# HGRN2's level loop: the second operand of each product copied by ScalarE, q multiplied beside k; retention's fourfold copies in one instruction

## The chip, the core and the metric

The kernel runs on one core of a Trainium2 chip. A core has five engines that run side by side and meet at semaphores: TensorE (PE, matrix products; its weight loads are shown apart as PEld), VectorE (DVE), ScalarE (ACT), GpSimd (POOL) and SyncE (SP, which here issues the transfers between the main memory and the core). The metric is the time of one execution on the device in microseconds; of several runs the median is taken.

## The reference

One step of a decoder trunk with two layers, width 2048, over 256 prompt tokens and 8 sequences of 4 sample tokens each; the kernel treats them as 288 columns. Layer 0 mixes by retention (4 heads) beside an RG-LRU, layer 1 by HGRN2 (16 heads of 128). After each mixer and each convolutional FFN stands a layer norm. For one HGRN2 head the reference computes, with `fg` the forget gate and `k = 1 - fg`:

```python
S_t = diag(f_t) S_{t-1} + k_t v_t^T ;  o_t = S_t^T q_t
# in chunks, b = cumsum(log f):
A = einsum('bhtk,bhsk,bhtsk->bhts', q, k, exp(b_t - b_s))      # s <= t
o = einsum('bhts,bhsv->bhtv', A, v) + einsum('bhtk,bhkv->bhtv', q * exp(b), S)
```

Retention computes `(q k^T * decay) v + q S` in the same way with a fixed decay for each head, and a new state. All inputs and outputs are float32.

## The kernel before

**Products.** Activations lie feature by feature: 16 tiles of 128 features by 288 columns. The weights stream from the main memory in chunks of 16 tiles of 128x128. ScalarE rounds half a chunk (8 tiles, 128x1024) to a high part `wh`, VectorE subtracts to get the low part `wl` (`split_hi`, `split_lo`); both are made some chunks of 8 ahead of their use. `gemm` sends three products for a weight tile (high by high, high by low, low by high) of 288 columns each.

**Order of the work.** The order of each engine's instructions is that in which the program is written, for TensorE, VectorE, ScalarE and GpSimd. The work of the heads is written as generators. After each weight tile `gemm` calls `tasks.tick()`, which lets one due generator go on; `yield n` means: not before n further ticks. So the distance between two steps of a head, in weight tiles on TensorE, is what stands in the `yield`s (`GAP_A`, `GAP_B`, `STAGE`), or more where several generators are due at once. An engine that has to wait for a semaphore holds up all that is written behind it on that engine.

**HGRN2's levels.** The triangle of a head's decayed scores `A` is built in seven levels, L = 1, 2, 4 to 64, after its diagonal. At level L the columns stand in blocks of 2L. Keys of a block's early half meet queries of its late half. Both have been multiplied with the gates between them and the block's middle, and the totals `T` of the gates are halved in number at each level. The prompt's second chunk of 128 columns runs backwards, so that one product serves both chunks. In a level (`levels`):

- `gather(i)`: ScalarE copies the early halves of k into the packed tile `E` (128x128).
- `scores(i)`: TensorE multiplies `E` with the late halves of q, read in place with a strided pattern (`late_half`), into a PSUM tile `hl`. At L = 2 a small second product serves the sample columns.
- VectorE multiplies k's early halves by the totals, makes the next totals `T`, and, after `yield GAP_A`, multiplies q's late halves (L1291); both in place.
- `keep(i)`: VectorE copies the valid scores under a mask into `AA` (L1255). Then comes `gather(i + 1)`, then `yield GAP_B + slow`, where `slow` is 1 in heads 0 and 1 and otherwise 0.

Since q is multiplied in place, VectorE may do it only when the product has read it, and the next product needs it done. After the levels follow transposes, state products and the output product `hpo`, which reads `AA`. A head takes 48 weight tiles (64 from head 7 on, where the gate's product stands beside it), so in heads 0 to 7 the tail of a head runs beside the levels of the next.

**Retention.** `vals` and `ret_inner` write the 32 sample columns of values and keys four times side by side into `v4` and `k4` on GpSimd, by four copies of 128x32 for each of two tiles; transposes on TensorE (`pst`) read them.

Of the kernel before, what the change touches and what calls it, by code (L numbers as in the profile page):

```python
# [10 lines left out]
F32 = mybir.dt.float32  # L11
F32R = mybir.dt.float32r
U32 = mybir.dt.uint32
AF = mybir.ActivationFunctionType
ALU = mybir.AluOpType
# [3 lines left out]
P = 128  # L19
D = 2048  # L20
KT = D // P
TP = 256
NB = 8
NS = 4
TS = NB * NS
T = TP + TS
# [18 lines left out]
LEAD_S = 3  # L45
STAGE = 4
D0 = 8
G0 = 0
GAP_A = 2
GAP_B = 2  # L50
R0 = 14
# [154 lines left out]
def early_half(t, L):  # L206

    return bass.AP(t.tensor, t.offset, [list(t.ap[0]), [2 * L, P // (2 * L)], [P + L, 2], [1, L]])


def late_half(t, L, c_first):

    n, c = [2 * L, P // (2 * L)], [P - L, 2]
    return bass.AP(t.tensor, t.offset + L, [list(t.ap[0])] + ([c, n] if c_first else [n, c]) + [[1, L]])


def totals(t, L, late):

    nb = P // (2 * L)
    o, c = (1, 2 * nb - 1) if late else (0, 2 * nb + 1)  # L220
    return bass.AP(t.tensor, t.offset + o, [list(t.ap[0]), [2, nb], [c, 2], [0, L]])
# [31 lines left out]
def build(tc, A, phases="ACDF"):  # L253
    nc = tc.nc
    V = nc.vector
    S = nc.scalar
    G = nc.gpsimd
# [7 lines left out]
    with contextlib.ExitStack() as est:  # L265
# [9 lines left out]
        def psx(name):  # L275
            return px.tile([P, 512], F32, tag="px", name=name)

        def mm(o, l, r, start=True, stop=True):
            return nc.tensor.matmul(o, l, r, start=start, stop=stop, skip_group_check=True)  # L279

        def tr(o, i):
            return nc.tensor.transpose(o, i, ident[:, :P])
# [26 lines left out]
        class Stream:  # L309
# [5 lines left out]
            cur = {}  # L315
# [454 lines left out]
        def even_in(eo, ea, o_rg, o_rt, prev, norm):  # L770
# [49 lines left out]
            def rope(h, nm, ms):  # L820
                a = [ea.tile([P, T], F32, name=f"{nm}{i}_{h}", tag=f"{nm}{i}") for i in range(2)]
                b = [ea.tile([P, T], F32, name=f"{nm}b{i}_{h}", tag=f"rb{i}") for i in range(2)]
                for i in range(2):
                    gemm("ev_in", ks, [ms[i]], xh, xl, done=lambda m, ps: rope_a(ps, a, b, i))
                return a

            def vals(h):
                vt = [ea.tile([P, T], F32, name=f"vt{i}_{h}", tag=f"vt{i}") for i in range(2)]
                v4 = ea.tile([P, 2 * 4 * TS], F32, name=f"v4_{h}", tag="v4")
                v44 = v4.rearrange("p (n r t) -> p n r t", n=2, r=4)  # L830

                def vdone(m, ps):
                    i = m - 16 - 2 * h
                    S.activation(vt[i], ps[:, :T], AF.Copy)
                    for r in range(4):
                        G.tensor_copy(v44[:, i, r, :], vt[i][:, TP:T])

                for i in range(2):
                    gemm("ev_in", ks, [16 + 2 * h + i], xh, xl, done=vdone)
                return vt, v4  # L840
# [98 lines left out]
            with tc.tile_pool(name="rt", bufs=1) as rt:  # L939
                for h in range(H_RET):  # L940
# [9 lines left out]
                    kk = rope(h, "k", [8 + 2 * h, 9 + 2 * h]) if h else kk0  # L950
# [3 lines left out]
                    vt, v4 = vals(h) if h else vv0  # L954
# [40 lines left out]
        def ret_inner(rt, h, cv, kk, qq, hd):  # L995
            zp = cv("zp")
            k4 = rt.tile([P, 2 * 4 * TS], F32, name=f"k4_{h}", tag="k4")
            k44 = k4.rearrange("p (n r t) -> p n r t", n=2, r=4)
            for kt in range(2):
                for r in range(4):  # L1000
                    G.tensor_copy(k44[:, kt, r, :], kk[kt][:, TP:T])
            hd["k4"] = k4
            a0 = psx(f"pa0_{h}")
            a1 = psx(f"pa1_{h}")
            for kt in range(2):
                mm(a0[:, :TP], kk[kt][:, 0:P], qq[kt][:, 0:TP], start=(kt == 0), stop=(kt == 1))
            for kt in range(2):
                mm(a1[:, :P], kk[kt][:, P:TP], qq[kt][:, P:TP], start=(kt == 0), stop=(kt == 1))
            for kt in range(2):
                mm(a1[:TS, P:P + TS], kk[kt][:, TP:T], qq[kt][:, TP:T], start=(kt == 0), stop=(kt == 1))  # L1010
            hd["A0"] = A0 = rt.tile([P, TP], F32, name=f"A0_{h}", tag="A0")
            hd["A1"] = A1 = rt.tile([P, P], F32, name=f"A1_{h}", tag="A1")
            hd["As"] = As = rt.tile([TS, TS], F32, name=f"As_{h}", tag="As")
            V.tensor_tensor(A0, a0[:, :TP], cv(f"dm{h}"), op=ALU.mult)
            V.tensor_tensor(A1, a1[:, :P], cv(f"dm{h}")[:, :P], op=ALU.mult)
            V.tensor_tensor(As, a1[:TS, P:P + TS], cv(f"dms{h}")[:TS], op=ALU.mult)
            hd["qx"] = qx = [rt.tile([P, TS], F32, name=f"qx{kt}_{h}", tag=f"qx{kt}") for kt in range(2)]
            for kt in range(2):
                V.tensor_tensor(qx[kt], qq[kt][:, TP:T], cv("xi")[:, h * TS:(h + 1) * TS], op=ALU.mult)
            yield 5  # L1020
            hd["ktk"] = ktk = [rt.tile([P, 256], F32, name=f"ktk{j}_{h}", tag=f"ktk{j}") for j in range(2)]
            for j in range(2):
                pk = psx(f"pkt{h}_{j}")
                for kt in range(2):
                    tr(pk[:, kt * P:(kt + 1) * P], kk[kt][:, j * P:(j + 1) * P])
                S.activation(ktk[j], pk[:, :256], AF.Copy, scale=zp[:, 2 * h + j:2 * h + j + 1])
# [148 lines left out]
        class HG:  # L1175
# [8 lines left out]
            def tl(self, nm, shape=(P, T), dt=F32, bufs=2):  # L1184
                return self.od.tile(list(shape), dt, name=f"{nm}_{self.h}", tag=nm, bufs=bufs)
# [48 lines left out]

            def gather(self, i):

                self.e = self.od.tile([P, P], F32, name=f"E{i}_{self.h}", tag="E", bufs=3)
                cut = lambda a: a.rearrange("p (n c l) -> p n c l", c=2, l=1 << i)
                S.activation(cut(self.e), early_half(self.k, 1 << i), AF.Copy)

            def scores(self, i):

                L = 1 << i
                self.ps = ps = psx(f"hl{self.h}_{i}")
                mm(ps[:, :P], self.e, late_half(self.qc, L, True))
                if L == 2:
                    late = self.qc[:, TP:].rearrange("p (n s l) -> p n s l", s=2, l=L)[:, :, 1, :]
                    mm(ps[:, P:P + TS // 2], self.k[:, T - P:], late)
# [15 lines left out]

            def levels(self):
                h, tl, k, qc = self.h, self.tl, self.k, self.qc
                slow = 1 if h < 2 else 0
                self.AA = tl("AA", (P, TP))
                k4 = tl("hk4", (P, P))
                self.gather(0)  # L1270
# [2 lines left out]
                cur = self.f  # L1273
                for i in range(7):
                    L = 1 << i
                    self.scores(i)
                    early, late = early_half(k, L), late_half(qc, L, False)
                    V.tensor_tensor(early, early, totals(cur, L, True), op=ALU.mult)
                    W = T if L <= 2 else TP
                    nb = W // (2 * L)  # L1280
                    tv = cur[:, :2 * nb].rearrange("p (n s) -> p n s", s=2)
                    if L <= 2:
                        n0 = TP // (2 * L)
                        ks = k[:, TP:T].rearrange("p (n s l) -> p n s l", s=2, l=L)[:, :, 0, :]
                        qs = qc[:, TP:T].rearrange("p (n s l) -> p n s l", s=2, l=L)[:, :, 1, :]
                        bc = lambda j: tv[:, n0:nb, j:j + 1].to_broadcast([P, nb - n0, L])
                        V.tensor_tensor(ks, ks, bc(1), op=ALU.mult)
                    nt = tl(f"T{i}", (P, nb))
                    V.tensor_tensor(nt, tv[:, :, 0], tv[:, :, 1], op=ALU.mult)
                    yield GAP_A + (G0 if i == 0 else 0)  # L1290
                    V.tensor_tensor(late, late, totals(cur, L, False), op=ALU.mult)  # L1291
                    if L <= 2:
                        V.tensor_tensor(qs, qs, bc(0), op=ALU.mult)
                    self.keep(i)
                    if L == 2:
                        self.t4 = nt[:, TP // 4:T // 4]
                    cur = nt
                    if i < 6:
                        self.gather(i + 1)
                    yield GAP_B + slow  # L1300
                self.tot = cur
                G.tensor_copy(k4.rearrange("p (r t) -> p r t", r=4), k[:, TP:T].unsqueeze(1).to_broadcast([P, 4, TS]))
                qm = self.qms[h % 2]
# [17 lines left out]
                kt = tl("kt", (P, 2 * P))  # L1321
# [8 lines left out]
                for b in range(NB):  # L1330
                    r = slice(32 * (b % 4), 32 * (b % 4) + TS)
# [51 lines left out]
                for j in range(2):  # L1383
                    pn = psx(f"hpn{h}_{j}")
                    c = slice(j * 512, (j + 1) * 512)
# [123 lines left out]
        for ph in phases:  # L1509
            i = "ACDF".index(ph)  # L1510
# [111 lines left out]
```

## Time and profile before

| | |
|---|---|
| median of 3 runs | 2830.85 us (2830.67 to 2831.03) |
| the profiled execution | 2834.14 us, its span 2832.2 us |
| busy: PE, DVE, ACT, POOL | 98%, 62%, 45%, 20% of the span |
| weights and states from the main memory | 450.71 MB read |
| L1239 copies `E`, x112 | 35.4 us on ScalarE |
| L1291 multiplications of q by totals, x96 | 31.8 us on VectorE |

An instruction's row names its line, engine and operation, and the tile written and those read (`out<-in`, buffer numbers left out). What ended an idle time of its engine stands behind `<-`. TensorE's instructions are pipelined: one starts before the one ahead of it has ended, so lengths overlap. A float32 product is drawn as two passes.

### The profile page before, as it was taken

What the parts mean: (1) busy time and instruction counts of PE and PEld (TensorE: products, weight loads), DVE (VectorE), ACT (ScalarE), POOL (GpSimd) and SP (SyncE); (2) the same over time, 40 slices, a digit from 0 to 9 for tenths busy, and PEclk for the clock granted to TensorE, in tenths of its full rate; (3) what the DMA queues carried; (4) which work ended last, traced back from release to release, by engine and by line L of the source; (5) the groups of instructions that cost most, each with busy time, mean ns of one, the idle gap of its engine ahead of it and who ended that gap; (6) DMA issues with size and microseconds to landing.
All of it is one profiled execution on the core that took longest, in us unless ns stands there. A gap on an engine that the chain in (4) does not pass through costs nothing.

```text
span 2832.2 us, 51174 instructions
## 1 busy us (share of the span) xinstructions
PE 2786.0 (98%) x21068; PEld 2752.9 (97%) x21068; DVE 1745.1 (62%) x2683; ACT 1277.2 (45%) x2234; POOL 556.7 (20%) x975
## 2 busy tenths in 40 slices
PE   9999999999999999999999999999999999999997
PEld 9999999999999999999999999999999999999997
DVE  7665566854554554558777766676854555554556
ACT  6534445643343443445555545555643443433433
POOL 1411024510000000007332222244400000000016
PEclk9999999999999999999999999999999999999998
DMA  6465444444444445445444444444444444444442
GB/s 250 165 242 201 182 167 167 159 170 164 164 164 165 171 156 177 166 160 182 148 151 161 167 167 155 166 158 162 164 164 172 171 151 177 164 164 168 167 166 90
DMA packets 80153, 476.20 MB, mean 168 GB/s; under 512 B 9392, under 2 KB 17840, under 8 KB 28208
## 3 DMA queue, kind: packets, MB, share of 16 engines
q1 hardware_dynamic: 79920, 472.94, 46.6%
q8 instruction: 165, 2.70, 0.4%
q14 instruction: 68, 0.56, 0.1%
HBM read 450.71 MB, written 22.19 MB: 167 GB/s over the span
## 4 chain that ended last, share of the span: by engine, by line
PE 88%; DVE 6%; ACT 2%; POOL 2%; issue 1%; DMA 0%; SPq 0%; DVEq 0%; ACTq 0%; POOLq 0%
PE ps_up L279 36%; PE ps_dn L279 18%; PE ps_od_in L279 12%; PE ps_ev_in L279 9%; PE ps_ev_out L279 4%; PE ps_od_out L279 4%; DVE wl L352 2%; PE hl L279 1%; DVE xl L580 1%; ACT wh L342 1%; PE hpo L279 1%; DVE xl L415 1%; DVE x L608 1%; PE po L279 0%; PE hpS L279 0%
## 5 line engine op out<-in xcount | busy, mean ns | idle before, releaser
L352 DVE TENSOR_TENSOR wl<-wr,wh 128x1024 fp32r<-128x1024 f32 (+1 forms) x818 | 1024.4, 1258 | 145.8 <-ACT wh L342 71.5
L342 ACT ACTIVATE wh<-wr 128x1024 fp32r<-128x1024 f32 (+1 forms) x818 | 845.5, 1049 | 352.8 <-PE ps_dn L279 294.1
L279 PE MATMUL ps_up<-xl,wh 128*128 128x288 f32 (+1 forms) x2816 | 832.8, 296 | 2.7 <-DVE xl L415 2.1
L279 PE MATMUL ps_up<-xh,wh 128*128 128x288 f32 (+1 forms) x2816 | 831.6, 295 | 3.2 <-ACT vs L405 3.2
L279 PE MATMUL ps_up<-xh,wl 128*128 128x288 f32 (+1 forms) x2816 | 831.7, 295 | 0.0
L279 PEld LDWEIGHTS ps_up<-xh,wh 128*128 128x128 f32 x2816 | 530.4, 188 | 3.8 <-ACT vs L405 3.7
L279 PEld LDWEIGHTS ps_up<-xl,wh 128*128 128x128 f32 x2816 | 529.5, 188 | 4.2 <-DVE xl L415 3.1
L279 PEld LDWEIGHTS ps_up<-xh,wl 128*128 128x128 f32 x2816 | 530.8, 188 | 0.0
L279 PE MATMUL ps_dn<-hh,wh 128*128 128x288 f32 x1408 | 417.4, 296 | 0.0
L279 PE MATMUL ps_dn<-hl,wh 128*128 128x288 f32 x1408 | 416.7, 296 | 0.0
L279 PE MATMUL ps_dn<-hh,wl 128*128 128x288 f32 x1408 | 415.1, 295 | 0.0
L279 PE MATMUL ps_od_in<-xh,wh 128*128 128x288 f32 (+1 forms) x1024 | 320.1, 313 | 0.1
L279 PE MATMUL ps_od_in<-xl,wh 128*128 128x288 f32 (+1 forms) x1024 | 302.8, 296 | 2.8 <-DVE xl L415 2.8
L279 PE MATMUL ps_od_in<-xh,wl 128*128 128x288 f32 (+1 forms) x1024 | 302.3, 295 | 0.0
L1415 POOL COPY fco<-us 128x2 f32<-128x2 f32 x88 | 18.4, 209 | 1367.3 <-ACT us L403 1367.3
L279 PEld LDWEIGHTS ps_dn<-hl,wh 128*128 128x128 f32 x1408 | 265.7, 189 | 0.1
L279 PEld LDWEIGHTS ps_dn<-hh,wl 128*128 128x128 f32 x1408 | 265.8, 189 | 0.0
L279 PEld LDWEIGHTS ps_dn<-hh,wh 128*128 128x128 f32 x1408 | 265.1, 188 | 0.1
L279 PE MATMUL ps_ev_in<-xh,wh 128*128 128x288 f32 x768 | 234.2, 305 | 0.3 <-ACT wh L342 0.3
L279 PE MATMUL ps_ev_in<-xh,wl 128*128 128x288 f32 x768 | 228.3, 297 | 0.5 <-DVE wl L352 0.5
L279 PE MATMUL ps_ev_in<-xl,wh 128*128 128x288 f32 x768 | 228.3, 297 | 0.0
L279 PEld LDWEIGHTS ps_od_in<-xl,wh 128*128 128x128 f32 x1024 | 193.6, 189 | 5.0 <-DVE xl L415 3.7
(316 smaller groups left out, 3913.7 us busy)
## 6 DMA issues: line engine op xcount, KB each, us to landing
wr<-w SPq DMA_DIRECT2D x404, 1024.0 KB, 4.8
s<-sret SPq DMA_DIRECT2D x16, 512.0 KB, 6.0
rs<-s SPq DMA_DIRECT2D x16, 512.0 KB, 4.7
hs<-shg SPq DMA_DIRECT2D x16, 512.0 KB, 5.6
gs<-hs SPq DMA_DIRECT2D x16, 512.0 KB, 2.6
wr<-w SPq DMA_DIRECT2D x6, 512.0 KB, 5.9
x<-x SPq DMA_DIRECT2D x16, 144.0 KB, 5.1
y<-x SPq DMA_DIRECT2D x16, 144.0 KB, 1.8
```

Of the source, the lines that this page charges most:

```text
L279: return nc.tensor.matmul(o, l, r, start=start, stop=stop, skip_group_check=True)
L342: S.activation(hi[:, d], src, AF.Copy)
L352: V.tensor_tensor(lo[:, d], src, hi[:, d].bitcast(F32), op=ALU.subtract)
L415: (eng or V).tensor_tensor(xl[k], src, xh[k].bitcast(F32), op=ALU.subtract)
L580: V.scalar_tensor_tensor(xl[k], x[k], self.col("lng", k), xh[k].bitcast(F32), ALU.mult, ALU.subtract)
L608: (G if i in MUG else V).tensor_tensor(x[k], x[k], self.rs, op=ALU.mult)
L1415: G.tensor_copy(fc4[:, f, 0, :], s[:, TP:TP + 2])
```

## The change

In the levels, `gather` makes a second packed copy: ScalarE copies the late halves of q into a tile `L`, and `scores` multiplies `E` with `L` and reads q no more (the small product at L = 2 still reads q and k in place). So VectorE's multiplication of q stands right behind that of k. `scores(i)` moves from the beginning of a level to `GAP_A` ticks behind the gathering for the next level, except at L = 2, where it stays at the beginning; `keep(i)` moves to the end. `E` and `L` have four buffers each (before: `E` three). The extra tick of heads 0 and 1 goes. In retention the four copies become one, whose input is read four times by a pattern of step 0.

```diff
--- before.py
+++ after.py
@@ -45,7 +45,6 @@
 LEAD_S = 3
 STAGE = 4
 D0 = 8
-G0 = 0
 GAP_A = 2
 GAP_B = 2
 R0 = 14
@@ -832,8 +831,7 @@
                 def vdone(m, ps):
                     i = m - 16 - 2 * h
                     S.activation(vt[i], ps[:, :T], AF.Copy)
-                    for r in range(4):
-                        G.tensor_copy(v44[:, i, r, :], vt[i][:, TP:T])
+                    G.tensor_copy(v44[:, i], vt[i][:, TP:T].unsqueeze(1).to_broadcast([P, 4, TS]))
 
                 for i in range(2):
                     gemm("ev_in", ks, [16 + 2 * h + i], xh, xl, done=vdone)
@@ -997,8 +995,7 @@
             k4 = rt.tile([P, 2 * 4 * TS], F32, name=f"k4_{h}", tag="k4")
             k44 = k4.rearrange("p (n r t) -> p n r t", n=2, r=4)
             for kt in range(2):
-                for r in range(4):
-                    G.tensor_copy(k44[:, kt, r, :], kk[kt][:, TP:T])
+                G.tensor_copy(k44[:, kt], kk[kt][:, TP:T].unsqueeze(1).to_broadcast([P, 4, TS]))
             hd["k4"] = k4
             a0 = psx(f"pa0_{h}")
             a1 = psx(f"pa1_{h}")
@@ -1234,15 +1231,18 @@
 
             def gather(self, i):
 
-                self.e = self.od.tile([P, P], F32, name=f"E{i}_{self.h}", tag="E", bufs=3)
-                cut = lambda a: a.rearrange("p (n c l) -> p n c l", c=2, l=1 << i)
-                S.activation(cut(self.e), early_half(self.k, 1 << i), AF.Copy)
+                L = 1 << i
+                self.e[i], self.l[i] = [self.od.tile([P, P], F32, name=f"{n}{i}_{self.h}", tag=n, bufs=4) for n in "EL"]
+                cut = lambda a: a.rearrange("p (n c l) -> p n c l", c=2, l=L)
+                S.activation(cut(self.e[i]), early_half(self.k, L), AF.Copy)
+                cut = lambda a: a.rearrange("p (c n l) -> p c n l", c=2, l=L)
+                S.activation(cut(self.l[i]), late_half(self.qc, L, True), AF.Copy)
 
             def scores(self, i):
 
                 L = 1 << i
                 self.ps = ps = psx(f"hl{self.h}_{i}")
-                mm(ps[:, :P], self.e, late_half(self.qc, L, True))
+                mm(ps[:, :P], self.e.pop(i), self.l.pop(i))
                 if L == 2:
                     late = self.qc[:, TP:].rearrange("p (n s l) -> p n s l", s=2, l=L)[:, :, 1, :]
                     mm(ps[:, P:P + TS // 2], self.k[:, T - P:], late)
@@ -1264,7 +1264,7 @@
 
             def levels(self):
                 h, tl, k, qc = self.h, self.tl, self.k, self.qc
-                slow = 1 if h < 2 else 0
+                self.e, self.l = {}, {}
                 self.AA = tl("AA", (P, TP))
                 k4 = tl("hk4", (P, P))
                 self.gather(0)
@@ -1273,9 +1273,11 @@
                 cur = self.f
                 for i in range(7):
                     L = 1 << i
-                    self.scores(i)
+                    if L == 2:
+                        self.scores(i)
                     early, late = early_half(k, L), late_half(qc, L, False)
                     V.tensor_tensor(early, early, totals(cur, L, True), op=ALU.mult)
+                    V.tensor_tensor(late, late, totals(cur, L, False), op=ALU.mult)
                     W = T if L <= 2 else TP
                     nb = W // (2 * L)
                     tv = cur[:, :2 * nb].rearrange("p (n s) -> p n s", s=2)
@@ -1285,19 +1287,19 @@
                         qs = qc[:, TP:T].rearrange("p (n s l) -> p n s l", s=2, l=L)[:, :, 1, :]
                         bc = lambda j: tv[:, n0:nb, j:j + 1].to_broadcast([P, nb - n0, L])
                         V.tensor_tensor(ks, ks, bc(1), op=ALU.mult)
+                        V.tensor_tensor(qs, qs, bc(0), op=ALU.mult)
                     nt = tl(f"T{i}", (P, nb))
                     V.tensor_tensor(nt, tv[:, :, 0], tv[:, :, 1], op=ALU.mult)
-                    yield GAP_A + (G0 if i == 0 else 0)
-                    V.tensor_tensor(late, late, totals(cur, L, False), op=ALU.mult)
-                    if L <= 2:
-                        V.tensor_tensor(qs, qs, bc(0), op=ALU.mult)
-                    self.keep(i)
                     if L == 2:
                         self.t4 = nt[:, TP // 4:T // 4]
                     cur = nt
                     if i < 6:
                         self.gather(i + 1)
-                    yield GAP_B + slow
+                    yield GAP_A
+                    if L != 2:
+                        self.scores(i)
+                    yield GAP_B
+                    self.keep(i)
                 self.tot = cur
                 G.tensor_copy(k4.rearrange("p (r t) -> p r t", r=4), k[:, TP:T].unsqueeze(1).to_broadcast([P, 4, TS]))
                 qm = self.qms[h % 2]
```

On VectorE, head 10 from the multiplication of k at level 1 to the next masked copy, before (k_10 and q_10 are keys and queries, T the totals, wl481 a weight split, AA the scores):

```order
L1278 TENSOR_TENSOR k_10_18620<-k_10_18620,T0_10_18765 128x32x2x2
L1287 TENSOR_TENSOR k_10_18620<-k_10_18620,T0_10_18765 128x8x2
L1289 TENSOR_TENSOR T1_10_18793<-T0_10_18765 128x72
L352 TENSOR_TENSOR wl481_18800<-wr240_18692,wh481_18731 128x1024
L1291 TENSOR_TENSOR q_10_18689<-q_10_18689,T0_10_18765 128x32x2x2
L1293 TENSOR_TENSOR q_10_18689<-q_10_18689,T0_10_18765 128x8x2
L1255 COPY_PREDICATED AA_10_18744<-lm_14338,hl10_1_18788 128x2x32x2
```

And the same stretch in the changed kernel:

```order
L1279 TENSOR_TENSOR k_10_18709<-k_10_18709,T0_10_18856 128x32x2x2
L1280 TENSOR_TENSOR q_10_18781<-q_10_18781,T0_10_18856 128x32x2x2
L1289 TENSOR_TENSOR k_10_18709<-k_10_18709,T0_10_18856 128x8x2
L1290 TENSOR_TENSOR q_10_18781<-q_10_18781,T0_10_18856 128x8x2
L1292 TENSOR_TENSOR T1_10_18888<-T0_10_18856 128x72
L351 TENSOR_TENSOR wl481_18905<-wr240_18784,wh481_18826 128x1024
L1255 COPY_PREDICATED AA_10_18833<-lm_14290,hl10_1_18881 128x2x32x2
```

The multiplication of q has moved from behind the weight split wl481 to right behind that of k; the split follows them.

On ScalarE, head 10 from its first copy, before (wh482 is a weight copy, v_10 the values):

```order
L1239 ACTIVATE E0_10_18746<-k_10_18620 128x128
L1239 ACTIVATE E1_10_18780<-k_10_18620 128x128
L342 ACTIVATE wh482_18798<-wr241_18796 128x1024
L403 ACTIVATE v_10_18805<-ps_od_in_42_0_18691 128x288
L403 ACTIVATE v_10_18805<-ps_od_in_42_0_18691 128x128
L1239 ACTIVATE E2_10_18815<-k_10_18620 128x128
```

And in the changed kernel:

```order
L1237 ACTIVATE E0_10_18835<-k_10_18709 128x128
L1239 ACTIVATE L0_10_18836<-q_10_18781 128x128
L1237 ACTIVATE E1_10_18858<-k_10_18709 128x128
L1239 ACTIVATE L1_10_18859<-q_10_18781 128x128
L1237 ACTIVATE E2_10_18890<-k_10_18709 128x128
L1239 ACTIVATE L2_10_18891<-q_10_18781 128x128
L402 ACTIVATE v_10_18897<-ps_od_in_42_0_18783 128x288
L402 ACTIVATE v_10_18897<-ps_od_in_42_0_18783 128x128
L341 ACTIVATE wh482_18903<-wr241_18901 128x1024
```

Each copy E is followed by a copy L of the queries, and the weight copy wh482 has moved behind v_10.

On TensorE the products of head 10 stood 2 tiles behind the diagonal, 4 tiles and a state product (hpn9_1) further, and then 4 tiles apart. Now product 0 stands 4 tiles and that state product behind the diagonal, product 1 follows it after 2 tiles, product 2 after 6, and from there on each after 4.

## Rows read from the trace of the kernel before

**Rows 1.** The page: busy time, share of the span, instructions by engine.

```profile
PE 2786.0 (98%) x21068; PEld 2752.9 (97%) x21068; DVE 1745.1 (62%) x2683; ACT 1277.2 (45%) x2234; POOL 556.7 (20%) x975
```

**Rows 2.** Stretch of the heads: engines' busy us, TensorE clock, DMA share, GB/s.

```profile
1390.00:1860.00 470.00, 458.82 (x3655) 445.82 (x3654) 332.64 (x863) 239.68 (x578) 125.58 (x140) 1.00 0.45 160
```

**Rows 3.** Tile E on TensorE: ns min/median/max; idle us before it, times, by cause.

```profile
L279 PE MATMUL hl<-q,E x224: 269/275/381, 1397.9 to 1849.5; 128*128 128x128 f32 x112
...
  DVE q L1293: 4.3, 9
  DVE q L1291: 3.6, 7
  ACT E L1239: 2.6, 5
```

**Rows 4.** Timeline, TensorE, head 4: start us, length us, instruction, [idle before].

```profile
1504.34 0.39 PE L279 MATMUL hl<-q,E 128*128 128x128 f32 x2
...
1505.89 0.29 PE L279 MATMUL ps_od_in<-xl,wh 128*128 128x288 f32 x1
...
1506.02 0.30 PE L279 MATMUL ps_od_in<-xh,wl 128*128 128x288 f32 x1
...
1507.14 0.49 PE L279 MATMUL hl<-q,E 128*128 128x128 f32 x2 [0.83 <-ACT E L1239]
```

**Rows 5.** Timeline, TensorE, head 10, products of levels 1 and 2.

```profile
1686.88 0.47 PE L279 MATMUL hl<-q,E 128*128 128x128 f32 x2
...
1687.18 0.29 PE L279 MATMUL hl<-q,k 128*128 128x16 f32 x2
...
1689.67 0.46 PE L279 MATMUL hl<-q,E 128*128 128x128 f32 x2 [0.53 <-DVE q L1293]
```

**Rows 6.** Timeline, VectorE, head 10, levels 1 and 2.

```profile
1687.58 0.29 DVE L1278 TENSOR_TENSOR k<-k,T 128x128 f32<-128x128 f32 x1 [0.48 <-PE hl L279]
...
1688.02 1.22 DVE L352 TENSOR_TENSOR wl<-wr,wh 128x1024 fp32r<-128x1024 f32 x1
...
1689.15 0.38 DVE L1291 TENSOR_TENSOR q<-q,T 128x128 f32<-128x128 f32 x1
...
1689.54 0.43 DVE L1255 COPY_PREDICATED AA<-lm,hl 128x128 f32<-128x128 uint32 x1
```

**Rows 7.** Timeline, ScalarE, head 10, weight copy and v.

```profile
1685.59 1.05 ACT L342 ACTIVATE wh<-wr 128x1024 fp32r<-128x1024 f32 x1
1686.92 0.72 ACT L403 ACTIVATE v<-ps_od_in 128x288 f32<-128x288 f32 x2 [0.28 <-PE ps_od_in L279]
```

**Rows 8.** Tile E on ScalarE: ns min/median/max, first and last start.

```profile
L1239 ACT ACTIVATE E<-k x112: 289/311/364, 1395.2 to 1848.0; 128x128 f32<-128x128 f32 x112
```

**Rows 9.** Groups on VectorE, 1330 to 1900: busy us, mean ns, idle before.

```profile
L1255 DVE COPY_PREDICATED AA<-lm,hl 128x128 f32<-128x128 uint32 x112 | 37.7, 336 | 0.8
...
L1291 DVE TENSOR_TENSOR q<-q,T 128x128 f32<-128x128 f32 x96 | 31.8, 332 | 12.1 <-PE hl L279 12.0
```

**Rows 10.** Timeline, head 5: VectorE, then GpSimd.

```profile
1535.89 1.98 DVE L1291 TENSOR_TENSOR q<-q,T 128x128 f32<-128x128 f32 x1
...
1535.75 1.97 POOL L1381 TENSOR_TENSOR hs<-hs,T 128x1024 f32<-128x1024 f32 x1
```

**Rows 11.** Timeline, TensorE, retention head 0.

```profile
121.04 0.33 PE L282 MATMUL pst<-ident,k 128*128 128x128 f32 x1 [2.14 <-POOL k L1001]
```

**Rows 12.** Timeline, GpSimd, before that.

```profile
109.86 3.23 POOL L836 COPY v<-vt 128x32 f32<-128x32 f32 x4
...
116.57 0.64 POOL L836 COPY v<-vt 128x32 f32<-128x32 f32 x4
...
120.35 1.22 POOL L1001 COPY k<-k 128x32 f32<-128x32 f32 x8
```

**Rows 13.** Tile hv on GpSimd: ns min/median/max.

```profile
L1220 POOL COPY hv<-v x16: 284/290/1389, 1400.7 to 1853.5; 128x128 f32<-128x128 f32 x16
```

**Rows 14.** Timeline, VectorE, weight splits beside those copies.

```profile
110.67 3.49 DVE L352 TENSOR_TENSOR wl<-wr,wh 128x1024 fp32r<-128x1024 f32 x3
```

## The prediction

> **What bounds the kernel now.** I read the page first: TensorE is busy 98% of the span [rows 1]. So a microsecond counts only where TensorE stands still. Next I cut the span into stretches. Between 1390 and 1860 us, where the 16 HGRN2 heads run, TensorE is busy 458.82 of 470.00 us, VectorE 333 and ScalarE 240, at full clock [rows 2]. The helpers are not short of cycles there; what is missing is a result at a moment.
>
> Then I asked for the tile that the level products read. Of TensorE's 11.2 us of visible idle in that stretch, 10.5 us in 21 waits stand before the products `hl<-q,E`: 7.9 us ended by a multiplication of q on VectorE, 2.6 by a copy E on ScalarE [rows 3]. The visible idle is not the whole wait. The timeline shows why: matmuls start 0.13 us apart but are drawn 0.30 long, so a product that started 1.12 us after its predecessor lost 0.99, of which its row shows 0.83. And the pair of passes of a late product is drawn 0.49 instead of 0.39 long, another 0.1 [rows 4]. So each visible wait costs about 0.16 + 0.08 more: 10.5 + 21 x 0.24 = 15.5 us, and 0.7 for the rest of the idle. Waits under 0.16 us show no idle at all, only the longer pair (0.47 at 1686.88, [rows 5]); I put a dozen of them at 0.18 each, 2.2 us. **What the levels can give: 18.4 us.**
>
> **The change part by part.**
>
> *Steady heads.* Heads 8 to 14 repeat one pattern; head 10 stands for them. TensorE starts the products of its levels 1 and 2 at 1686.88 and 1689.67, and waits 0.53 us visibly at level 2 [rows 5]. VectorE shows the cause: k is multiplied at 1687.58, then a weight split of 1.22 us is in the way, and only at 1689.15 comes q, which the product reads directly [rows 6]. Now q follows k at once, ahead of that split, and product 2 stands 6 weight tiles behind product 1 instead of 4. A tile is three matmuls, 0.39 us. Counted from the second product of level 1 (1687.18): k starts at +0.40 as before, q at about +0.6 and is over at +0.9; copy E runs beside q, and the new copy L from about +0.95 to +1.26. The product is due at 0.22 + 6 x 0.39 = +2.56. **Margin 1.3 us where there was a wait.** Level 1: product 1 keeps its six tiles behind hl_d, and q no longer stands behind the addition into hs that came between; its small wait goes too. The tightest is level 3: VectorE does k, q, two short pieces, T and the split until about +2.35, the masked copies until about +3.0 (0.43 for the large one, half of that for the small one, an estimate from its size), then k, and q until about +3.5. ScalarE has meanwhile v (0.72) and a weight copy (1.05) [rows 7], until +3.0, so E starts at about +3.35 and L ends at +4.0; product 3 is due at 2.56 + 0.22 + 4 x 0.39 = +4.35. Margin 0.35. Later levels have 4 tiles each and no v: more.
>
> *What is added.* 112 copies L. No row shows one; the copies E, of the same size and gathered in the same way, take 289 to 364 ns [rows 8]. The ends I keep are 0.29 us, that fastest E, and 1.05 us, a whole weight copy [rows 7]. I take 0.31, the median of E. That is 35 us more ScalarE in a stretch where it idles 230; at 0.31 it lies beside TensorE wholly. If that cover were gone, each copy would stand in front of its product: 35 us. Behind a waiting L on ScalarE stand the weight copies and the copies of v; weights are split three chunks of 8 tiles, some 9 us, ahead of their use, so a microsecond is not felt. VectorE's multiplication of q now waits for L where it waited for the product (12.0 us in all, [rows 9]); the wait for the product passes to the masked copy, whose result nothing on TensorE reads soon.
>
> *Crowded heads.* In heads 0 to 7 the tail of one head overlaps the levels of the next. There a long wait has another cause: at 1535.89 a q multiplication took 1.98 us, where these take about 0.33 [rows 9], while GpSimd ran hs<-hs,T (1535.75, 1.97 us) [rows 10]; its product came as late. Moving q does not remove such a meeting, only gives it one or two tiles (0.4 to 0.8 us) of slack. I leave 1.5 us for them and 1.5 us for misses at level 3 elsewhere. **Levels: 18.4 - 3 = 15.4 us.**
>
> *Heads 0 and 1 lose one tile of spacing per level.* Their levels end 7 tiles sooner. The longer distance from copy to product hides that, so I cost it at nothing; if it does not, their share of the waits stays (some 2 us).
>
> *Packed operand.* The products read L contiguously. The fastest passes of the group are 269 ns, the median 275 [rows 3]: 224 x 6 ns = 1.3 us is the most that packing gives, and I count none.
>
> *Retention's copies on GpSimd.* TensorE waits for them at one place: `pst<-ident,k`, 2.14 us at 121.04 [rows 11]. Ahead of it GpSimd works without a pause from 105 us on: four copies of v take 3.23 us, the next four 0.64, and eight of k 1.22 [rows 12]. One 128x128 copy takes 290 ns at the median of the hv row, 1.39 us at most [rows 13]. By these rows alone the saving in front of pst is (3.23 - 0.29) + (0.64 - 0.29) + (0.61 - 0.29) = 3.6, more than the wait. But three splits of VectorE fill 110.67 to 114.16 [rows 14], just where the copies took a microsecond apiece. With three copies fewer, the small operations behind them meet the same splits, and I let GpSimd be only three such operations (3 x 0.12, by the 0.64 for four copies at most 0.16 each) further at 114.2: 0.4 + 0.35 + 0.35 = 1.1, and 0.1 from the second pst. **1.2 us**, bounds 0.7 and 2.3. The Trainium skill has this as a rule ("SBUF — State Buffer", Who interferes with whom): VectorE and GpSimd share a port pair as an exclusive lock, and a VectorE instruction with two SBUF inputs blocks a GpSimd one that reads SBUF until it ends. The rows agree; by the rule the small figure holds, by the rows' difference the whole wait would go. The other three retention heads show no such wait.
>
> *DMA queue.* A few weight loads change places by one on SyncE. The DMA engines are busy under half of the time [rows 2]; nothing.
>
> **Sum.** 15.4 + 1.2 = 16.6 us. The profiled execution took 2834.14 us (span 2832.2), so it would take 2817.5. The median of the runs shown is 2830.85, 3.3 us lower; at the same distance it comes to 2814.2. I say **2814 us**.
>
> **Rivals.**
>
> *Only the steady heads gain.* There one wait of 0.53 + 0.24 and a short one per head, about 1.0 us, seven heads: 7 us, and 1.2 in retention: 2834.14 - 8.2 - 3.3 = 2822.6. For it: the meeting of [rows 10], and more work in ScalarE's queue in crowded heads. Against it: the added distance holds in every head.
>
> *The wait moves.* If VectorE's whole backlog is the cause and not its order, each product waits as long as before, now for L; only retention's 1.2 remains: 2829.6. Against it: VectorE idles 137 us of the 470 [rows 2], and in head 10 one split in the wrong place accounts for the wait.
>
> *Slower: L on the path at every level.* Place: ScalarE's queue. VectorE's q of the next level waits for L, which waits for q of this one and for a weight copy ahead of it. It decides once masked copy, k, q and L with that weight copy take longer than a level's 4 tiles and its product, 1.57 + 0.22 = 1.8 us. By the means they take 0.34 + 0.33 + 0.33 [rows 9] + 0.31 = 1.3, and 2.4 with a weight copy in line, at every second level: 3.7 for two levels against 3.6. So it would just decide if nothing overlapped; but weight copies run while VectorE works. If it decides, 112 x 0.31 = 35 us come and 18.4 go: 2847.
>
> *More than forecast.* All 18.4 and 2.3: 2830.85 - 20.7 = 2810.
>
> **How the numbers follow.** Forecast 0.62 (2811 to 2819), steady heads only 0.17, wait moves 0.10, slower 0.05, more 0.06. A measurement of this kernel can tell about 0.2% (5.7 us): faster means below 2825.2. Forecast and upper case are faster, the steady case mostly (0.12 of 0.17): 0.80. Same: the rest of it and most of the moved wait, 0.14. Slower: 0.06. The range runs from the upper case to just above the steady case, 2810 to 2824. At the 0.29 us end of L nothing changes; at the 1.05 end level 3 is late by 0.74 - 0.35 in 16 heads, 6 us: 2820, inside it.
>
> **What would show it.** In the changed profile the products should show under 2 us of idle where there were 11.2, no q among what ends it, and ScalarE a group L x112 of about 0.31 us; VectorE's wait for the products should stand at the masked copy; pst should wait about 1 us. I am wrong if products wait for L in the steady heads, or if VectorE's k and q wait for ScalarE by tens of us and weights come late to TensorE.

## The result, and the profile after

The changed kernel took **2812.11 us** (median of 4 runs, 2811.9 to 2813.4); the kernel before took 2830.94 beside it (4 runs, 2830.67 to 2831.97). The ratio is 0.9932, interval 0.9917 to 0.9948: 18.8 us less. The forecast was 2814, between 2810 and 2824.

The page of the changed kernel, busy time by engine, against [rows 1]:

```profile
PE 2777.9 (99%) x21068; PEld 2750.5 (98%) x21068; DVE 1738.0 (62%) x2683; ACT 1300.8 (46%) x2346; POOL 536.7 (19%) x927
```

TensorE runs the same 21068 matmuls and is drawn busy for 8 us less. Most of that was no work: 5 us are the parts of the waits that the busy rows hide (21 waits at 0.24, as the prediction counted them), 1.5 a stretch at half clock told of at the end. ScalarE has 112 instructions more, GpSimd 48 fewer.

The stretch of the heads, columns as in [rows 2]:

```profile
1390.00:1860.00 470.00, 469.73 (x3792) 461.20 (x3791) 340.39 (x880) 273.50 (x713) 118.90 (x144) 1.00 0.46 164
```

TensorE's visible idle there fell from 11.2 us to 0.3, while ScalarE became 34 us busier. The products' tile on TensorE, against [rows 3]:

```profile
L278 PE MATMUL hl<-L,E x224: 270/273/378, 1393.5 to 1828.1; 128*128 128x128 f32 x112
its engine sat idle before it (us, times) until:
who waited for it (us, times):
  DVE AA L1255: 11.3, 17
```

Nothing stands under "sat idle": of the 21 visible waits none is left. Someone waits for the products now, the masked copy into AA on VectorE. Counted without the drawing (start of each product minus the start of the matmul ahead, less the usual 0.13, and its second pass less 0.11), the products lost 18.7 us before and lose 2.1 now: **16.6 us gained.**

The new copies on ScalarE, against the copies E of [rows 8]:

```profile
L1239 ACT ACTIVATE L<-q x112: 292/297/327, 1390.3 to 1827.0; 128x128 f32<-128x128 f32 x112
```

Groups on VectorE from 1320 to 1890, against [rows 9]:

```profile
L1255 DVE COPY_PREDICATED AA<-lm,hl 128x128 f32<-128x128 uint32 x112 | 38.1, 340 | 11.9 <-PE hl L278 11.3
...
L1280 DVE TENSOR_TENSOR q<-q,T 128x128 f32<-128x128 f32 x96 | 30.7, 320 | 0.0
```

The wait for the products has moved as a whole from the multiplication of q (12.1 us before) to the masked copy (0.8 before). It costs VectorE the same and TensorE nothing.

Head 10, level 2 to 3, on VectorE, against [rows 6]:

```profile
1670.03 0.33 DVE L1279 TENSOR_TENSOR k<-k,T 128x128 f32<-128x128 f32 x1
1670.28 0.27 DVE L1280 TENSOR_TENSOR q<-q,T 128x128 f32<-128x128 f32 x1
...
1670.79 1.21 DVE L351 TENSOR_TENSOR wl<-wr,wh 128x1024 fp32r<-128x1024 f32 x1
```

The split that stood between k and q now stands behind both. ScalarE in the same head, against [rows 7]:

```profile
1668.88 0.32 ACT L1239 ACTIVATE L<-q 128x128 f32<-128x128 f32 x1
...
1670.39 0.31 ACT L1237 ACTIVATE E<-k 128x128 f32<-128x128 f32 x1 [1.19 <-DVE k L1279]
1670.61 0.29 ACT L1239 ACTIVATE L<-q 128x128 f32<-128x128 f32 x1
1670.81 0.70 ACT L402 ACTIVATE v<-ps_od_in 128x288 f32<-128x288 f32 x2
1671.40 1.05 ACT L341 ACTIVATE wh<-wr 128x1024 fp32r<-128x1024 f32 x1
1672.94 0.31 ACT L1237 ACTIVATE E<-k 128x128 f32<-128x128 f32 x1 [0.49 <-DVE k L1279]
1673.16 0.30 ACT L1239 ACTIVATE L<-q 128x128 f32<-128x128 f32 x1
```

And TensorE's products of levels 1, 2 and 3, against [rows 5]:

```profile
1669.26 0.49 PE L278 MATMUL hl<-L,E 128*128 128x128 f32 x2
1669.58 0.29 PE L278 MATMUL hl<-q,k 128*128 128x16 f32 x2
...
1672.18 0.38 PE L278 MATMUL hl<-L,E 128*128 128x128 f32 x2
...
1674.01 0.39 PE L278 MATMUL hl<-L,E 128*128 128x128 f32 x2
```

Read the margins from where L ends to where its product starts. Level 2: 1670.90 to 1672.18, 1.28 us. Level 3: 1673.46 to 1674.01, 0.55. Level 1: L ends at 1669.20, the product starts 0.17 behind the matmul ahead of it and is drawn 0.49 instead of 0.38: it is still a little late.

Retention head 0, TensorE, against [rows 11], and GpSimd, against [rows 12]:

```profile
120.77 0.33 PE L281 MATMUL pst<-ident,k 128*128 128x128 f32 x1 [1.11 <-POOL k L998]
```

```profile
110.59 0.28 POOL L834 COPY v<-vt 128x128 f32<-128x128 f32 x1
110.82 0.69 POOL L562 CAST xh<-gbh 128x2 fp32r<-128x2 f32 x1
111.46 1.24 POOL L563 CAST xl<-gbl 128x2 fp32r<-128x2 f32 x1
112.64 1.19 POOL L562 CAST xh<-gbh 128x2 fp32r<-128x2 f32 x1
113.78 1.19 POOL L563 CAST xl<-gbl 128x2 fp32r<-128x2 f32 x1
114.91 0.18 POOL L920 COPY rgh<-org 128x1 f32<-128x1 f32 x1
...
116.99 0.28 POOL L834 COPY v<-vt 128x128 f32<-128x128 f32 x1
...
120.43 0.51 POOL L998 COPY k<-k 128x128 f32<-128x128 f32 x2
```

VectorE beside it, against [rows 14]:

```profile
111.46 3.46 DVE L351 TENSOR_TENSOR wl<-wr,wh 128x1024 fp32r<-128x1024 f32 x3
```

The copies shrank, the wait only by half. The three GpSimd operations that now meet the splits take 1.19 to 1.24 us, where the same kinds take 0.18 elsewhere; the one ahead of them, 0.69, stands beside a scan of VectorE that ends at 111.53. The Trainium skill's rule ("SBUF — State Buffer", Who interferes with whom), by which a VectorE instruction with two SBUF inputs blocks a GpSimd one that reads SBUF, agrees: the operations caught there end about when the splits do, whatever they are, and behind the last split they take 0.18 again.

### The profile page after: what moved, and what is told of

Same layout as the page of the kernel before. It is cut to its first block, busy times and chain, and to the rows that moved or that the text cites. A ratio compares the mean times of both kernels' runs of the same rounds, so it can differ in the third digit from the quotient of the medians.

```text
span 2810.4 us, 51235 instructions
## 1 busy us (share of the span) xinstructions
PE 2777.9 (99%) x21068; PEld 2750.5 (98%) x21068; DVE 1738.0 (62%) x2683; ACT 1300.8 (46%) x2346; POOL 536.7 (19%) x927
## 4 chain that ended last, share of the span: by engine, by line
PE 92%; DVE 6%; ACT 1%; issue 1%; POOL 1%; DMA 0%; SPq 0%; DVEq 0%; ACTq 0%
PE ps_up L278 36%; PE ps_dn L278 18%; PE ps_od_in L278 13%; PE ps_ev_in L278 11%; PE ps_ev_out L278 4%; PE ps_od_out L278 4%; DVE wl L351 2%; PE hl L278 1%; DVE xl L579 1%; PE hpo L278 1%; DVE x L607 1%; DVE xl L414 1%; PE po L278 0%; PE hpS L278 0%; PE hl_d L278 0%
## 5 line engine op out<-in xcount | busy, mean ns | idle before, releaser
L402 ACT ACTIVATE us<-ps_up 128x256 f32<-128x256 f32 (+1 forms) x176 | 41.7, 290 | 346.1 <-PE ps_up L278 346.1
```

Source lines behind the costliest of these rows:

```text
L402: S.activation(o, ps[:, c], func)
```

## The experiments

Two theories. **A**, the prediction's: TensorE waited because a result was late by its place in a queue; order and distance remove that, the copies are what allows them, and retention's gain is separate. **B**: some one part does it (the order alone, the copies alone), or the margins are so thin that a little more work on ScalarE gives the gain back. The kernel before took 2831.2 to 2831.5 us in these runs; ratios are against it.

**e1: the kernel before again.** No edit.

> The kernel before, profiled a second time. The two profiles differ by 22 us, the medians by 18.8, so 3.2 us of the first profile of before are not the change. Theory (order): the waits of the level products repeat, 10.5 us of visible idle give or take 1; the 2.1 us wait of pst repeats; what is missing this time is in the two places that the new order does not touch: the waits for xl near 1380 us (2.2 us there, 0.7 in the changed kernel) and the stretch of 3.4 us at half clock behind pst (1.6 us). Rival (the profile of before was lucky or unlucky in the products): their idle changes by 3 us or more. Time about 2831.

2829.8 us (one run), span 2827.8. The waits before the products come back to the tenth (q 4.3 in 9 and 3.7 in 7 waits, E 2.6 in 5), and pst waits 2.17. They belong to the program. What did not come back are 4.4 us in two other places, told of below.

**e2: the levels alone.** The changed kernel with retention's four copies put back:

```
-  G.tensor_copy(k44[:, kt], kk[kt][:, TP:T].unsqueeze(1).to_broadcast([P, 4, TS]))
+  for r in range(4):
+      G.tensor_copy(k44[:, kt, r, :], kk[kt][:, TP:T])      (and so for v44)
```

> The changed levels, retention's copies as before (four each). Theory: 2831 - 16.6 = 2814.3, products with under 1 us of visible idle, pst waiting 2.1 us again. Rival (retention's copies carry more than their wait, through the half clock behind it): 2816 or more. Rival (levels are not the cause): over 2825.

2814.33 us, ratio 0.9941 (0.9929 to 0.9953): 16.9 us less. No product waits visibly; pst waits 2.2 as before. It takes 2.2 us more than the changed kernel. In its profile 1.4 of that stand at pst, and 1.1 at retention head 1, where two matmuls `pc<-s,qx` wait for the state's transfer (0.27 and 0.46 us visible); the profiles of before and e1, with the same copies, don't have that wait.

**e3: retention alone.** The kernel before with the one-piece copies.

> The kernel before with retention's copies in one piece, levels as before. Theory: 1.2 us less, 2829.7, pst waiting about 1 us instead of 2.1. Rival (half clock behind pst goes with the shorter wait in every execution): 2.5 to 3 us less, 2828. Rival (no effect): 2831.

2828.35 us, ratio 0.9989 (0.998 to 0.9998): 2.9 us less, an interval from 0.6 to 5.7. The products wait as before, pst 1.1. In the profiles the time from the start of the matmul ahead of pst to pst is 2.39 to 2.44 us in five profiles with four copies (before, e1, e2, e4, e5) and 1.35 to 1.41 in five with one piece (after, e3, e6, e7, e12; e11 has 1.41 too); the second pst's 0.3 goes too. So 1.0 + 0.3 in the traces. But the time, 2828.35, lies on the rival's 2828 and not on 2829.7, and the interval holds both. The rival's ground doesn't hold as it stands, since e1 has the long wait without the half clock. Against e1's profiled execution (2829.8) that of e3 (2827.83) is 2.0 us shorter, 1.4 of them at pst. Where the rest of the 2.9 comes from is not shown; the half clock of some executions (last section) may be part of it. The two parts together (16.9 and 2.9) give the whole within the intervals.

**e4: the copies alone.** The kernel before, L gathered beside E, old order and old distance:

```
+  S.activation(cut(self.l), late_half(self.qc, L, True), AF.Copy)
-  mm(ps[:, :P], self.e, late_half(self.qc, L, True))
+  mm(ps[:, :P], self.e, self.l)
```

> The kernel before with the copies L added and the products reading them, but all in the old order: q multiplied GAP_A behind k, both copies behind it, product 2 tiles later. Theory (order and distance win the time, the copy alone costs): each product that waited for q now waits for q and L, some 0.35 us more for 34 products, and more products wait: 12 to 25 us above before, 2843 to 2856. Rival (the packed operand, or q freed from the product, is what wins): at or below 2831.

2837.77 us, ratio 1.0025 (1.0014 to 1.0035): 6.6 us **more**. Its products' tile says why:

```profile
its engine sat idle before it (us, times) until:
  ACT L L1242: 15.7, 28
```

28 visible waits where there were 21. By starts the products lose 25.2 us, 6.5 over before, which is the measured loss. The sign was as expected, the size was not (2843 at least): I had added 0.35 us to each of 34 late products. In heads 9 to 14 a late product lost 0.27 more (0.50 for 0.23 at level 1, 1.04 for 0.77 at level 2): before, it had waited for the small piece behind q [rows 5], which L doesn't wait for. Only a few products became late that had been in time, and one wait of 1.7 us in head 5 went. Copies in the old order only lengthen the chain k, q, L, product.

**e5: the order alone.** The kernel before with q right behind k and no copies:

```
   V.tensor_tensor(early, early, totals(cur, L, True), op=ALU.mult)
+  V.tensor_tensor(late, late, totals(cur, L, False), op=ALU.mult)
   ...
-  yield GAP_A + (G0 if i == 0 else 0)
-  V.tensor_tensor(late, late, totals(cur, L, False), op=ALU.mult)
-  self.keep(i)
   ...
-  yield GAP_B + slow
+  yield GAP_A
+  yield GAP_B
+  self.keep(i)
```

> No copies L: the products read q in place at the beginning of their level as before, but q is multiplied right behind k and the masked copy stands at the end of the level; products 4 tiles apart. No change in retention. Theory (the order on VectorE is the larger part, the copies buy the rest of the distance): most of the waits go, some 6 us of 18 stay, 2817 to 2822; in head 10 product 2 waits no more and product 3 waits 0.2 to 0.3 us. Rival (without copies q must wait for the product, so nothing is won): 2829 or more. Rival (copies are superfluous): 2815 or less.

2819.86 us, ratio 0.9961 (0.9948 to 0.9975): 11.4 us less, 5.5 short of e2, which differs in the copies and the distance. Its products:

```profile
its engine sat idle before it (us, times) until:
  ACT E L1239: 2.3, 6
  DVE q L1288: 1.3, 2
who waited for it (us, times):
  DVE q L1278: 13.2, 18
```

By starts 8.5 us are lost (some 6 were expected). The last line shows the limit: the next level's multiplication of q overwrites what the product reads, so it waits for the product. That the product can't be put later without holding the chain up is reasoned from this line; no run puts it 6 tiles behind without the copies.

**e6: the distance undone.** The changed kernel with each product 4 tiles behind its copies:

```
-  yield GAP_A
   if L != 2:
       self.scores(i)
+  yield GAP_A
   yield GAP_B
```

> The changed kernel with each product moved 2 tiles ahead, right behind the gathering for the next level, so 4 tiles behind its own copies where the change has 6. Theory (the distance is what hides the copies): product 3 of the steady heads, with a margin of 0.35 us at 6 tiles, waits 0.4 to 0.5 us, the crowded heads more; some 10 us of waits return, 2819 to 2825, ended by L and E. Rival (q beside k suffices, the distance is idle): 2812 to 2814.

2820.98 us, ratio 0.9964 (0.9952 to 0.9977), 9 us over the changed kernel, as expected. Its products:

```profile
its engine sat idle before it (us, times) until:
  ACT L L1239: 4.9, 12
```

By starts 11.6 us; product 3 of heads 9 to 13 loses 0.42 to 0.43, where 0.4 to 0.5 was expected. The kernel has the copies and still loses more at its products than e5, which has none. **So the copies bring nothing by themselves; they free q, and that lets the product stand later.** That is theory A, with the one step named under e5 left untried. (E's fourth buffer came with the copies in every run; e4 has it too and is slower, but it was not tried alone.)

**e7: each L copied twice.** Into the same tile, 34 us more on ScalarE:

```
   S.activation(cut(self.l[i]), late_half(self.qc, L, True), AF.Copy)
+  S.activation(cut(self.l[i]), late_half(self.qc, L, True), AF.Copy)
```

> The changed kernel with each copy L made twice into the same tile: 112 more copies, 34 us more ScalarE. Theory (the copies lie beside TensorE): 2812 to 2815, the small margins of level 3 giving up to 3 us of waits. Rival (ScalarE is close to the path): 2 products in 3 late by a copy, 20 to 35 us more, 2832 to 2847.

2817.89 us, ratio 0.9952 (0.9938 to 0.9965): 5.8 us over the changed kernel, outside what I expected. Its products, and the product of level 1 in head 10:

```profile
its engine sat idle before it (us, times) until:
  ACT L L1240: 3.1, 11
```

```profile
1673.81 0.38 PE L278 MATMUL hl<-L,E 128*128 128x128 f32 x1 [0.22 <-ACT L L1240]
```

By starts 7.5 us, 5.4 more. Most of them lie where the margin was smallest, at level 1: just under 0.5 us each in heads 9 to 14, and 0.5 to 0.8 in heads 1, 6 and 7. Other levels are late in heads 2 and 5, in one level of 14 and one of 15; in heads 8 to 13 they took the second copy without a trace. Theory B is right about level 1, and not about the 34 us.

**e8: pst four tiles later.** The changed kernel with retention's outer part started at `R0 + 14` instead of `R0 + 10`, so that the copies of k are there:

> The changed kernel with the second half of retention head 0, that begins with pvt and pst, started 4 weight tiles later (1.6 us). Theory (TensorE waits at pst only because it comes before GpSimd's copies, 1.1 us of visible idle): the wait goes, 1.3 us less, 2810.8. Rival (the wait moves to the next product that needs a result of this head): 2812.1.

2815.23 us, ratio 0.9943 (0.993 to 0.9955): not faster but some 3 us slower than the changed kernel. pst waits no more; another matmul does:

```profile
169.63 1.07 PE L278 MATMUL pc<-s,qx 128*32 128x256 f32 x16 [3.28 <-DMA s<-sret]
```

This is retention head 1, whose state is loaded into a buffer that head 0 gives back at its end. Head 0 ended later, so the load came later: SyncE issues its third part at 164.86 us, in the changed kernel at 159.73. The wait removed came back as a longer one.

**e9: GpSimd's queue cleared instead.** The changed kernel, with the 32 small casts of the norm's parameters (`xh<-gbh`, `xl<-gbl`) issued behind the preparation of the first retention head and not ahead of it:

```
-  if ph != phases[-1]:
+  if ph != phases[-1] and ph != "A":
       tasks.spawn(norm.cols(prev), 200)
   ...
   vv0 = vals(0)
   tasks.drain()
+  tasks.spawn(norm.cols(prev), 60)
```

> The changed kernel with the 32 small casts of the next norm's gains, which GpSimd does in one go right ahead of retention head 0's copies, handed out behind them; no step of the head moves. Theory (pst waits because GpSimd's queue is long, and nothing else is late): some 3 us sooner at the copies, the wait of pst goes, no new wait at pc, 1.3 us less than the change. Rival (the next product of the head waits instead): no difference. Rival (the casts fall where they delay others): slower.

**2809.82 us** (2809.73 to 2810.66, 5 runs), ratio 0.9925 (0.9912 to 0.9937), against 2811.52 of the changed kernel beside it (e12): 1.7 us better (1.3 forecast), with ranges that don't overlap. GpSimd and TensorE:

```profile
115.23 0.28 POOL L834 COPY v<-vt 128x128 f32<-128x128 f32 x1
115.46 0.52 POOL L999 COPY k<-k 128x128 f32<-128x128 f32 x2
```

```profile
118.67 0.27 PE L281 MATMUL pst<-ident,k 128*128 128x128 f32 x1
```

The copies of k start 3.2 us ahead of pst, which no longer waits. This version beats both kernels.

**e10: e9 with 7 tiles from copy to product** (`GAP_A` 3, `GAP_B` 1).

> As e9, and each product one more tile behind its copies, the masked copy one tile nearer (7 and 1 where the change has 6 and 2). Theory (2.1 us of hidden waits are left at the products): up to 1.5 us less than e9. Rival (VectorE now waits for the product at the masked copy and delays k and q): as e9 or up to 5 us more.

2809.71 us, ratio 0.9925 (0.9911 to 0.9938): the same as e9. By starts the products lose 1.3 us where they lost 2.0; VectorE's masked copies wait 15.8 us for them, in 24 waits. In head 7 an output matmul (`hpo<-sm,q`, 1590.86) now loses 0.9 us waiting for `sm`, a copy of ScalarE, and uses up the gain. Six tiles are enough here.

**e11: the spacing of heads 0 and 1 kept.** The changed kernel with the extra tile per level put back (`yield GAP_B + slow`).

> The changed kernel with the extra tile per level in heads 0 and 1 kept. Theory (the distance hides the closer spacing): as the change, within 1 us. Rival (VectorE's backlog in the first heads needs it): 1 to 2 us less.

2811.46 us, ratio 0.9929 (0.9916 to 0.9941), as the changed kernel (e12). Taking the extra tile away cost nothing; with it the profile even shows two waits for L, 1.1 us together, that e12 doesn't have.

**e12: the changed kernel again,** beside e9 to e11. No edit.

> The changed kernel again, as the base of the three others on this chip. All theories: 2811.5 to 2813.5, products without visible idle, pst waiting 1.1 us.

2811.52 us (2810.98 to 2813.14), ratio 0.9931 (0.9919 to 0.9943): the result stands.

## Why the prediction was right

- *What the levels can give: 18.4 us.* Right: 18.7 by starts at the products, where the forecast had 17.7 for them and 0.7 for other idle. The visible idle of 10.5 would have been far too little; adding 0.24 a wait and 2.2 for the ones that show no idle was needed.
- *Steady heads, margin 1.3 at level 2 and 0.35 at level 3.* Right: 1.28 and 0.55. The chain was followed well: E of level 3 was to start 3.35 us behind the second product of level 1, and starts at 1672.94, 3.36 behind 1669.58.
- *Level 1: its small wait goes too.* **Wrong.** In heads 9 to 14 that product is still some 0.13 late (0.49 in the row above). Its time runs from the masking of hl_d (the diagonal's product) through k, q, E and L, and L ends at the moment when it is due. It cost 0.8 us here, but it is the place where e7 lost half a microsecond per head.
- *Crowded heads keep 1.5 us, misses at level 3 another 1.5.* The first kind is there: the two largest waits left (0.4 each, heads 6 and 7) are at level 1. In head 6 a multiplication of k takes 1.22 us,

```profile
1545.82 1.22 DVE L1279 TENSOR_TENSOR k<-k,f 128x128 f32<-128x128 f32 x1
```

 while GpSimd adds into hs:

```profile
1544.88 1.90 POOL L1383 TENSOR_TENSOR hs<-hs,T 128x1024 f32<-128x1024 f32 x1
```

 Level 3 loses 0.04 us at most in a steady head. The 3 us left were 2.1: **levels 16.6 us measured, 15.4 forecast**, the term most off; it lies between the forecast and the case *more than forecast* (18.4).
- *Copies L: 0.31 us, hidden.* 0.297, and hidden but for the margin of level 1. That a 1.05 us copy would cost only 6 us was wrong: 0.3 us more cost 5.8 already (e7), because I looked at level 3 for the thinnest margin and it was at level 1.
- *The wait passes to the masked copy.* Right, 11.9 us there.
- *Heads 0 and 1, packed operand: nothing.* Right: e11, and a median pass of 273 ns for 275.
- *Retention 1.2 us, not the whole 2.3.* Right in the traces: 1.3 to 1.4, a visible wait of 1.1 left as said, and in the way that was told: when the splits end, GpSimd has four casts behind it where it had one, three operations more. In the times it is less clear: 2.2 us by e2, 2.9 by e3, with wide intervals.
- *Only the steady heads gain, the wait moves, L on the path:* fallen, the first two by e2 and the visible waits at nought; the third is what e4 does, where the order is the old one.
- *The step from the profiled 2834.14 to 2814.* I took the 3.3 us between the profile and the median off without knowing what they were. e1 shows that they don't come back in every execution, and that the profile had more of them: counted by starts, the profiled execution of before lost 4.4 us over e1's, in two places alone. 1.5 lie in the half clock behind pst, and 2.9 in the waits for xl near 1382 (1.65, 0.23 and 0.93 us visible, a single one of 0.63 in e1). The changed kernel's profile has neither (0.57 for xl). So profile against profile: 2834.14 - 18.0 (16.6 and 1.4) - 4.4 = 2811.7, against 2812.14. Taking something off was right, but the size was read from the medians and not understood. e4's profile has both losses too, no other has either; why they come together stays open.

## What to carry to other kernels

A visible wait is only part of a wait: count starts against the matmul ahead, and the small ones come to light. The copies that free an operand were worth nothing by themselves here; they were worth the distance they allow. So make the copy and move the reader in one step, and then look for the one reader that kept its old place (here level 1). Where a helper's result is late, look at what stands ahead of it in that helper's queue (e9) before the reader is moved (e8): a later reader gives its buffers back later too.

## What the runs showed of the hardware

In the profile of before, TensorE's granted clock fell behind pst. Stretch, length, busy time of PE, PEld, DVE, ACT and POOL, clock, DMA share, GB/s, before and then e1:

```profile
122.40:125.80 3.40, 3.40 (x16) 3.31 (x14) 3.00 (x5) 2.06 (x5) 0.00 (x0) 0.51 0.53 157
```

```profile
122.40:125.80 3.40, 3.40 (x41) 2.76 (x43) 2.99 (x5) 2.23 (x5) 0.00 (x0) 1.00 0.47 133
```

0.51 is the lower level, 1.2 GHz. TensorE had stood 2.14 us before it in the first and 2.17 in the second, so the same wait was followed by the lower clock once and not the other time; of five profiles with that wait, before and e4 have it, e1, e2 and e5 don't. It cost 1.5 us: 80 matmuls from pst on take 10.6 us with it and 9.0 without. None of the nine with a wait of 1.1 us or less there has it. So a short wait's price is not fixed, and part of the spread between runs of one kernel may lie there: beside each other, 15 executions of before ran from 2829.4 to 2834.99 us and 11 of e3 from 2827.73 to 2829.4. It is not shown, since only one execution of a run is profiled, and e2, with the long wait, stayed within 1 us.

And one copy of a 128x128 tile whose source is read four times takes 0.28 us on GpSimd, where four copies of 128x32 take 0.64 [rows 12], both away from VectorE's splits.
